# Layer 0's remaining modulation begins beside RWKV's first chunks instead of at once

## The chip, the cores and the metric

The kernel runs on one core of one Trainium2 chip. The metric is the device time of one execution in microseconds (us), less is better. One launch computes two layers.

## What is computed

The reference is a trunk of two layers over 512 latent tokens and 256 context tokens (T = 768) of 1024 channels. Each layer, in short:

```python
s_lat = jax.nn.silu(c)
s_ctx = jax.nn.silu(c_ctx)
...
for l in range(DEPTH):
    m_lat = jnp.split((s_lat @ w_mod[l] + b_mod[l])[:, None, :], 6, axis=-1)
    m_ctx = jnp.split((s_ctx @ w_mod[l] + b_mod[l])[None, None, :], 6, axis=-1)
    h_lat = _modulate(x_lat, m_lat[0], m_lat[1])       # x * (1 + scale) + shift
    ...
    y_ctx, y_lat = _mixing_sublayer(...)               # four mixers of one projection, gated and merged
    x_lat = _layer_norm(ALPHA * x_lat + m_lat[2] * y_lat, ln1_g[l], ln1_b[l])
    f_lat = _sq_relu_mlp(_modulate(x_lat, m_lat[3], m_lat[4]), w_ff1[l], w_ff2[l])
    x_lat = _layer_norm(ALPHA * x_lat + m_lat[5] * f_lat, ln2_g[l], ln2_b[l])
    ...
```

The mixers are mLSTM, RWKV-7, latent attention (MLA) and RG-LRU. The modulation depends on `c` and `c_ctx` alone. Shift 1 and scale 1 of a layer (blocks 0 to 3 of 512 columns each) are needed before its input projection; the other blocks, 4 to 11, only after its mixers.

## The kernel before

Tokens lie along the free axis, channels over the 128 partitions. A weight tile of 1024 x 128 (512 KB) is loaded on SP's queue into one of the buffers `wraw` (L343), split by ACT (`whi`, L302) and DVE (`wlo`, L303) into two parts, and multiplied in three passes into PSUM (`mm3`, all by L389). The modulation's loads use the same `wraw` buffers and the same queue.

**The modulation.** `modulation` (L430) lists 48 units for each layer: 12 blocks of 512 columns in 4 quarters of the input. Layer 0's blocks 0 to 3 come first, in `first_mod`, ahead of the mixers. `more_mod` (L442) takes units off the list; `mod_unit` (L447) does one: a load of 512 KB on SP (L450), then four operations on DVE that add weight x c into two accumulators `modacc`, one for the latent tokens' c and one for the context's (L458 starts a block, L460 goes on). With a block's last quarter, small matmuls of `modacc` with a column of ones sum over the partitions into `pq` (by L389), and DVE adds the bias (L498). Layer 0 has 32 units left when its mixers begin, 128 accumulations on DVE.

**The mixers.** `mixers` (L600) writes the program of four threads, one piece at a time: RWKV (`rwkv`, L1429), the modulation (`mod_thread`), the foreground (LRU, latent attention MLA, mLSTM, the gates, one after the other) and a filler. Each thread yields a latency. `now` is an estimate of PE's time, the sum of the work written so far; a thread is taken up again when `now` has passed the time at which it yielded plus its latency, and of the ready ones the first in the list goes. With `mpos=0` the modulation is the first. Its own first yield is `mstart`; then it writes one unit for each `mod=6.6` of `now`.

What is written in this way is then ordered for each engine by the scheduler of the framework, ahead of the run; on the chip each engine executes its own list in order and waits by semaphores. So a unit of the modulation can stand ahead of, or between, the DVE work of a mixer.

**The mixers' steps that the text speaks of.** In the LRU (L963 to L1005) ACT and DVE pass a tile back and forth (L980 and L985 on DVE, L982 to L991 on ACT, with DVE's L990 to L997 behind). RWKV's projections are evicted from PSUM by L1417 to L1419 on ACT and shifted on DVE (L1422, L1425); L1489 on DVE reads PSUM that the first product of the chunks needs (`kpz`). RWKV then goes through six groups of chunks; L1574 begins a group on DVE. Beside them runs MLA's softmax: DVE takes the row's largest (L1095) and scales it (L1096), ACT makes the exponential and its sum (L1098), DVE the reciprocal (L1100), POOL divides (`p`, L1101), and PE transposes the result (`pq`, L400). After the chunks RWKV's output is normed (`ky`, L1501 to L1512). The mLSTM works on two pairs of heads; at the end of each, DVE forms the output `hs` (L1353 to L1364) and its norm with ACT (L1384 to L1392, ACT's square L1388), and PE transposes it. ACT's decay exponentials `mde` (L1250) are the mLSTM's as well.

Of the kernel before, what the change touches and what calls it, by code (L numbers as in the profile page):

```python
# [137 lines left out]
def _layout(inp):  # L138
# [73 lines left out]
    for d in range(2):  # L212
        for gi, nm in enumerate(("lru_wa", "lru_wx")):
            for t in range(2):
# [22 lines left out]
PARM = (  # L237
         dict(rw0=0.3, rw1=0.1, lru=1.7, mla0=2, mla1=0.7, mlp=0.462, ml0=0.66, ml1=0.785, ga=4, sp=3, g3=10,
              g1=0.462, mod=6.6, left=219, left0=136, hr=0, hm=0, hf=0, hw=50, fm0=5, fm1=6, cs=1, dl=1, nr=1, lns=2,
              hl0=0, hl1=0, hl2=0, hres=0, hx=0, pw1=146, pw2=2, mpos=0, mstart=0),  # L240
         dict(rw0=0.099, rw1=0.3, lru=2.8, mla0=1.96, mla1=1.705, mlp=2.38, ml0=2.785, ml1=2.36, ga=2, sp=1.18,
              g3=10, g1=0.809, mod=16.8, left=146, left0=0, hr=0, hm=0, hf=0, hw=50, fm0=5, fm1=6, cs=0, dl=1, nr=0,
              lns=2, hl0=0, hl1=0, hl2=0, hres=0, hx=0, pw1=0, pw2=0, mpos=3, mstart=60),
# [1555 lines left out]
```

## Time and profile before

| | |
|---|---|
| median of 3 runs | 2747.7 us (2746.25 to 2752.73) |
| profiled execution | 2745.26 us, its span 2743.5 us |
| granted TensorE clock, mean | 0.974 of full speed |
| busy: PE, DVE, ACT, POOL | 2587.3, 1546.2, 1029.6, 441.8 us |
| DMA | 300.07 MB, 109 GB/s mean |

Busy shares are of the span. PE is TensorE, ACT the Scalar engine, DVE the Vector engine, POOL GpSimd, SP the queue that issues the DMAs. Layer 0's mixers begin at about 48 us of the span; RWKV's chunk groups begin at 182, 266.5, 333, 391.5, 454.5 and 507 us and end at 611.5; the first mLSTM pair ends near 656 us.

### The profile page before, as it was taken

How to read it: one execution, taken by the hardware profiler on the slowest of the kernel's cores; microseconds unless marked ns; L12 is line 12 of the kernel's file. 1: busy time of each engine (PE TensorE's matmuls, PEld its weight loads, DVE VectorE, ACT ScalarE, POOL GpSimd, SP SyncE). 2: the span in 40 equal slices, each digit the busy share in tenths (PEclk: the TensorE clock that was granted, in tenths of full speed). 3: DMA queues.
4: the chain of work that ended last, by engine and by line, in shares of the span. 5: the costliest groups of instructions: out<-in, count | busy, mean ns of one | idle time of the engine just before them, and what ended most of it. 6: DMA issues, size and time to landing. Idle time of an engine off the chain costs nothing. (4 is left out here: it accounts for less than half of the span.)

```text
span 2743.5 us, 53586 instructions
## 1 busy us (share of the span) xinstructions
PE 2587.3 (94%) x22980; PEld 2112.7 (77%) x22980; DVE 1546.2 (56%) x2627; ACT 1029.6 (38%) x1642; POOL 441.8 (16%) x420
## 2 busy tenths in 40 slices
PE   7999999998999999999999988999999899999997
PEld 4777776777888878888888867666776778888887
DVE  6885775554354377555553575565665355833335
ACT  3653334335222244121213366543433433622324
POOL 0110212211023132010202200111211113211111
PEclk9999998999999999999999999899999999999998
DMA  7452331133263323434342242211122356333333
GB/s 267 149 176 65 98 96 31 51 90 111 83 215 97 122 85 123 125 121 123 119 125 72 89 136 92 90 52 55 50 73 84 115 177 205 116 100 99 94 99 101
DMA packets 117581, 300.07 MB, mean 109 GB/s; under 512 B 11056, under 2 KB 38064, under 8 KB 117344
## 3 DMA queue, kind: packets, MB, share of 16 engines
q1 hardware_dynamic: 117344, 296.66, 34.1%
q8 instruction: 180, 2.95, 0.4%
q14 instruction: 57, 0.47, 0.1%
HBM read 261.60 MB, written 34.91 MB: 108 GB/s over the span
## 5 line engine op out<-in xcount | busy, mean ns | idle before, releaser
L302 ACT ACTIVATE whi<-wraw 128x1024 fp32r<-128x1024 f32 x295 | 312.0, 1058 | 957.0 <-PE m L389 718.4
L389 PE MATMUL m<-hhi,whi 128*128 128x256 f32 (+1 forms) x2000 | 601.6, 362 | 21.7 <-ACT mk L1273 5.9
L389 PE MATMUL m<-hlo,whi 128*128 128x256 f32 (+1 forms) x2000 | 591.0, 356 | 2.7 <-DVE hlo L921 2.1
L389 PE MATMUL m<-hhi,wlo 128*128 128x256 f32 (+1 forms) x2000 | 588.4, 355 | 0.7 <-DVE wlo L303 0.7
L303 DVE TENSOR_TENSOR wlo<-wraw,whi 128x1024 fp32r<-128x1024 f32 x291 | 367.8, 1265 | 382.3 <-ACT whi L302 371.6
L389 PEld LDWEIGHTS m<-hhi,whi 128*128 128x128 f32 x2000 | 379.0, 191 | 86.3 <-issue 8.2
L389 PEld LDWEIGHTS m<-hlo,whi 128*128 128x128 f32 x2000 | 381.1, 191 | 59.2 <-DVE hlo L921 4.7
L389 PEld LDWEIGHTS m<-hhi,wlo 128*128 128x128 f32 x2000 | 380.1, 191 | 55.6 <-issue 3.2
L460 DVE SCALAR_TENSOR_TENSOR modacc<-wraw,ccs,modacc 128x512 f32<-128x512 f32 x296 | 223.9, 805 | 41.1 <-DMA wraw<-wmod 41.1
L818 POOL TENSOR_TENSOR rl<-rl 128x512 f32<-128x512 f32 (+2 forms) x73 | 117.8, 1614 | 706.1 <-ACT rl L817 661.9
L389 PE MATMUL m<-fhi,whi 128*128 128x256 f32 (+1 forms) x608 | 175.8, 340 | 1.1 <-ACT fhi L302 1.1
L389 PE MATMUL m<-flo,whi 128*128 128x256 f32 (+1 forms) x608 | 175.5, 340 | 0.2 <-DVE flo L303 0.2
L389 PE MATMUL m<-fhi,wlo 128*128 128x256 f32 (+1 forms) x608 | 175.0, 339 | 0.0
L719 POOL TENSOR_TENSOR gth<-gth 128x768 f32<-128x768 f32 (+1 forms) x48 | 82.9, 1749 | 346.2 <-DVE gth L715 344.3
L794 DVE SCALAR_TENSOR_TENSOR x<-m,dvec,x 128x512 f32<-128x512 f32 (+1 forms) x92 | 53.9, 607 | 128.6 <-PE m L389 128.3
L389 PEld LDWEIGHTS m<-fhi,whi 128*128 128x128 f32 x608 | 113.7, 188 | 15.1 <-ACT fhi L302 1.3
L389 PEld LDWEIGHTS m<-flo,whi 128*128 128x128 f32 x608 | 114.3, 188 | 13.8 <-DVE flo L303 0.6
L389 PEld LDWEIGHTS m<-fhi,wlo 128*128 128x128 f32 x608 | 114.5, 188 | 13.4
L303 DVE TENSOR_TENSOR flo<-rl,fhi 128x512 fp32r<-128x512 f32 (+2 forms) x73 | 55.2, 757 | 82.7 <-ACT fhi L302 82.6
L302 ACT ACTIVATE fhi<-rl 128x512 fp32r<-128x512 f32 (+2 forms) x73 | 49.1, 673 | 112.8 <-POOL rl L818 112.8
L389 PE MATMUL m<-osp,whi 128*128 128x256 f32 (+1 forms) x328 | 79.6, 353 | 6.8 <-DVE osp L303 3.2
L1101 POOL TENSOR_SCALAR p<-p,fst 128x768 f32<-128x768 f32 (+1 forms) x40 | 40.4, 1010 | 250.3 <-DVE fst L1100 210.6
(436 smaller groups left out, 4407.9 us busy)
## 6 DMA issues: line engine op xcount, KB each, us to landing
wraw<-wf SPq DMA_DIRECT2D x145, 512.0 KB, 3.6
wraw<-win SPq DMA_DIRECT2D x106, 512.0 KB, 4.2
wraw<-wmod SPq DMA_DIRECT2D x85, 512.0 KB, 3.6
wraw<-wout SPq DMA_DIRECT2D x28, 512.0 KB, 3.7
kwin<-rkv SPq DMA_DIRECT2D x20, 512.0 KB
gd<-gth SPq DMA_DIRECT2D x23, 384.0 KB, 3.6
gth<-gd SPq DMA_DIRECT2D x23, 384.0 KB, 4.5
wraw<-wbr SPq DMA_DIRECT2D x16, 512.0 KB
```

The source lines that it names most:

```text
L302: self.nc.scalar.activation(hi, src, AF.Copy)
L303: (self.nc.gpsimd if pool else self.nc.vector).tensor_tensor(lo, src, hi.bitcast(F32), op=ALU.subtract)
L389: self.nc.tensor.matmul(out, lhsT=lhsT, rhs=rhs, start=start, stop=stop)
L460: nc.vector.scalar_tensor_tensor(acc, w, c, acc, op0=ALU.mult, op1=ALU.add)
L719: nc.gpsimd.tensor_tensor(self.z[dt][:, q0:T], self.z[dt][:, q0:T], th[:, q0:T], op=ALU.add)
L794: nc.vector.scalar_tensor_tensor(x[et][:, a:b], ps[:, a + off:b + off], gm[:, et, j:j + 1], x[et][:, a:b], op0=ALU.mult, op1=ALU.add)
L818: nc.gpsimd.tensor_tensor(rl[:, a:b], rl[:, a:b], rl[:, a:b], op=ALU.mult)
L1101: nc.gpsimd.tensor_scalar(p[:, 0:nk], p[:, 0:nk], st[:, 3:4], 0.0, op0=ALU.mult, op1=ALU.add)
```

## The change

One number: in layer 0's parameters (`PARM[0]`, L240) `mstart` goes from 0 to 110. The modulation's thread then waits until the other threads have written 110 us of PE work by the program's own estimate, and only then begins with its 32 units, one for each 6.6 us as before. What each unit does stays as it is.

```diff
--- before.py
+++ after.py
@@ -237,7 +237,7 @@
 PARM = (
          dict(rw0=0.3, rw1=0.1, lru=1.7, mla0=2, mla1=0.7, mlp=0.462, ml0=0.66, ml1=0.785, ga=4, sp=3, g3=10,
               g1=0.462, mod=6.6, left=219, left0=136, hr=0, hm=0, hf=0, hw=50, fm0=5, fm1=6, cs=1, dl=1, nr=1, lns=2,
-              hl0=0, hl1=0, hl2=0, hres=0, hx=0, pw1=146, pw2=2, mpos=0, mstart=0),
+              hl0=0, hl1=0, hl2=0, hres=0, hx=0, pw1=146, pw2=2, mpos=0, mstart=110),
          dict(rw0=0.099, rw1=0.3, lru=2.8, mla0=1.96, mla1=1.705, mlp=2.38, ml0=2.785, ml1=2.36, ga=2, sp=1.18,
               g3=10, g1=0.809, mod=16.8, left=146, left0=0, hr=0, hm=0, hf=0, hw=50, fm0=5, fm1=6, cs=0, dl=1, nr=0,
               lns=2, hl0=0, hl1=0, hl2=0, hres=0, hx=0, pw1=0, pw2=0, mpos=3, mstart=60),
```

The diff shows one number; the program that follows from it differs in the order of the instructions on each engine, from the start of the mixers to the second mLSTM pair. Three places on DVE show it. A row is line, operation, output, inputs and shape.

The first is early in the mixers, in the LRU's first half beside RWKV's projections; `ls`, `ltq` and `ll` are the LRU's tiles, `modacc` the modulation's, and - is before, + the change.

```order
 L1425 TENSOR_TENSOR cqgd<-cqgd,ktmp 128x512
-L460 SCALAR_TENSOR_TENSOR modacc<-wraw,ccs,modacc 128x512 x3
+L980 TENSOR_SCALAR ls<-lth,dvec 128x768
 L1452 TENSOR_SCALAR cqgd<-cqgd 64x768
-L980 TENSOR_SCALAR ls<-lth,dvec 128x768
-L460 SCALAR_TENSOR_TENSOR modacc<-wraw,ccs,modacc 128x512
-L303 TENSOR_TENSOR wlo<-wraw,whi 128x1024
 L985 TENSOR_SCALAR ltq<-ltq 128x768
-L460 SCALAR_TENSOR_TENSOR modacc<-wraw,ccs,modacc 128x512 x5
-L990 TENSOR_TENSOR ll_625<-ll_625,ltq 128x768
-L460 SCALAR_TENSOR_TENSOR modacc<-wraw,ccs,modacc 128x512
+L990 TENSOR_TENSOR ll_581<-ll_581,ltq 128x768
```

Ten accumulations (x3, one, x5, one) leave this stretch, five of them from right ahead of L990, and L980 moves up by one place.

The second is in RWKV's fourth chunk group, where MLA's softmax runs beside it; `fst` holds the softmax's row values, `kt` is RWKV's. Before:

```order
L1095 TENSOR_REDUCE fst<-m_4732 128x1
L1100 RECIPROCAL fst<-fst 128x1
L1689 TENSOR_TENSOR kt<-kp_4663,cst 128x256
L1096 TENSOR_SCALAR fst<-fst 128x1
L1095 TENSOR_REDUCE fst<-m_4882 128x1
L1096 TENSOR_SCALAR fst<-fst 128x1
L1694 TENSOR_TENSOR kt<-kt,kp_4697 128x256
L1100 RECIPROCAL fst<-fst 128x1
L1695 STREAM_TRANSPOSE kt<-kt 128x256
L1095 TENSOR_REDUCE fst<-m_4949 128x1
```

With the change, at the corresponding place:

```order
L1695 STREAM_TRANSPOSE kt<-kt 128x256
L460 SCALAR_TENSOR_TENSOR modacc<-wraw,ccs,modacc 128x512
L1095 TENSOR_REDUCE fst<-m_4911 128x1
L1689 TENSOR_TENSOR kt<-kp_4629,cst 128x256
L1096 TENSOR_SCALAR fst<-fst 128x1
L460 SCALAR_TENSOR_TENSOR modacc<-wraw,ccs,modacc 128x512 x2
L1694 TENSOR_TENSOR kt<-kt,kp_4663 128x256
L1100 RECIPROCAL fst<-fst 128x1
L460 SCALAR_TENSOR_TENSOR modacc<-wraw,ccs,modacc 128x512
L1695 STREAM_TRANSPOSE kt<-kt 128x256
L460 SCALAR_TENSOR_TENSOR modacc<-wraw,ccs,modacc 128x512
```

Accumulations now stand between L1096 and L1100 of a softmax row and ahead of the next row's L1095, where there were none.

The third is the end of the first mLSTM pair; `ky` and `kn` are RWKV's output and its norm, `hs`, `mht` and `mhn` the mLSTM's. Before:

```order
L1363 TENSOR_TENSOR mht<-pn,mdn 128x384
L1510 TENSOR_TENSOR ky<-ky,kn_7052 128x256
L1364 TENSOR_TENSOR hs<-hs,mht 128x384
L1512 TENSOR_TENSOR ky<-kpw,ky 128x256
L1509 SCALAR_TENSOR_TENSOR ky<-ky,vec_80,kn_7051 128x512
L1384 TENSOR_REDUCE mhn<-hs 128x12
L1510 TENSOR_TENSOR ky<-ky,kn_7052 128x512
L1385 TENSOR_SCALAR mhn<-mhn 128x12
L303 TENSOR_TENSOR wlo<-wraw,whi 128x1024
L1512 TENSOR_TENSOR ky<-kpw,ky 128x512
L1386 TENSOR_TENSOR hs<-hs,mhn 128x768
```

With the change:

```order
L1363 TENSOR_TENSOR mht<-pn,mdn 128x384
L1364 TENSOR_TENSOR hs<-hs,mht 128x384
L1384 TENSOR_REDUCE mhn<-hs 128x12
L1385 TENSOR_SCALAR mhn<-mhn 128x12
L1386 TENSOR_TENSOR hs<-hs,mhn 128x768
L1389 TENSOR_REDUCE mhn<-msq 128x12
L303 TENSOR_TENSOR wlo<-wraw,whi 128x1024
L1392 TENSOR_TENSOR hs<-hs,mhn 128x768
```

RWKV's rows of `ky` and a weight's `wlo` are no longer between L1363 and L1386; they stand ahead of them.

## Rows read from the trace of the kernel before

**Rows 1.** The page, busy time by engine and share of the span.

```profile
PE 2587.3 (94%) x22980; PEld 2112.7 (77%) x22980; DVE 1546.2 (56%) x2627; ACT 1029.6 (38%) x1642; POOL 441.8 (16%) x420
```

**Rows 2.** Windows, by stage: stretch, length, busy by engine (instructions), clock, DMA share, GB/s.

```profile
48.00:182.00 134.00, 123.56 (x696) 100.65 (x696) 116.06 (x163) 79.27 (x95) 14.24 (x29) 0.94 0.45 144
...
266.50:333.00 66.50, 59.57 (x1110) 46.38 (x1110) 53.64 (x116) 21.95 (x52) 12.50 (x12) 0.97 0.36 109
333.00:391.50 58.50, 53.85 (x1078) 42.36 (x1078) 41.31 (x98) 19.20 (x44) 10.54 (x11) 0.97 0.31 97
391.50:454.50 63.00, 59.44 (x1014) 42.90 (x1012) 38.58 (x86) 24.76 (x59) 10.89 (x14) 0.93 0.17 54
454.50:507.00 52.50, 48.72 (x1005) 37.56 (x1004) 28.63 (x79) 21.20 (x55) 11.79 (x14) 0.93 0.09 23
```

**Rows 3.** The same windows, tile modacc alone: PE, PEld, DVE, clock, DMA share, GB/s.

```profile
48.00:182.00 134.00, 3.46 (x96) 3.12 (x96) 44.97 (x64) 0.94 0.45 144
182.00:266.50 84.50, 2.16 (x64) 2.03 (x64) 10.43 (x17) 0.94 0.34 111
266.50:333.00 66.50, 1.14 (x34) 1.01 (x32) 22.43 (x32) 0.97 0.36 109
333.00:391.50 58.50, 2.15 (x64) 2.03 (x64) 10.59 (x16) 0.97 0.31 97
```

**Rows 4.** PE's waits, 48 to 182 us: releaser, us in total, times, longest.

```profile
PE m L389 <- ACT kwdad L1419: 3.9, 1, 3.9
PE m L389 <- ACT kk L1419: 2.5, 1, 2.5
```

**Rows 5.** Timeline, 82.5 to 91.2 us: start, length, instruction, idle before.

```profile
82.59 3.40 DVE L460 SCALAR_TENSOR_TENSOR modacc<-wraw,ccs,modacc 128x512 f32<-128x512 f32 x5
...
84.22 0.94 ACT L989 ACTIVATE ltq<-ltq,cbias 128x768 f32<-128x768 f32 x1
...
85.90 0.96 DVE L990 TENSOR_TENSOR ll<-ll,ltq 128x768 f32<-128x768 f32 x1
...
90.85 0.80 PE L389 MATMUL m<-xc,lruw 128*128 128x256 f32 x1 [3.94 <-ACT kwdad L1419]
```

**Rows 6.** Windows of 20 us, columns as in the windows by stage.

```profile
80.00:100.00 20.00, 16.06 (x69) 12.48 (x68) 17.80 (x23) 15.66 (x19) 2.04 (x1) 0.83 0.50 154
...
180.00:200.00 20.00, 17.90 (x108) 15.15 (x108) 14.81 (x31) 6.27 (x15) 3.31 (x3) 0.74 0.67 229
...
640.00:660.00 20.00, 13.20 (x66) 11.24 (x65) 14.11 (x17) 15.09 (x34) 8.62 (x6) 0.84 0.45 141
```

**Rows 7.** PE's waits, 182 to 391.5 us.

```profile
PE pq L400 <- POOL p L1101: 7.3, 7, 2.9
PE kpz L389 <- DVE kr L1489: 2.3, 1, 2.3
```

**Rows 8.** PE's waits, 391.5 to 520 us.

```profile
PE pq L400 <- POOL p L1101: 0.3, 1, 0.3
```

**Rows 9.** Line L1101, 182 to 392 us: durations in ns, min/median/max.

```profile
L1101 POOL TENSOR_SCALAR p<-p,fst x10: 905/1346/2135, 257.4 to 371.2; 128x768 f32<-128x768 f32 x8, 128x256 f32<-128x256 f32 x2
```

**Rows 10.** Line L1101, 392 to 520 us.

```profile
L1101 POOL TENSOR_SCALAR p<-p,fst x13: 478/905/1742, 394.3 to 519.9; 128x768 f32<-128x768 f32 x8, 128x256 f32<-128x256 f32 x5
```

**Rows 11.** Timeline of DVE, end of the first mLSTM pair.

```profile
639.05 0.55 DVE L1363 TENSOR_TENSOR mht<-pn,mdn 128x384 f32<-128x384 f32 x1
...
641.18 2.22 DVE L1364 TENSOR_TENSOR hs<-hs,mht 128x384 f32<-128x384 f32 x1
...
647.58 0.94 DVE L1386 TENSOR_TENSOR hs<-hs,mhn 128x768 f32<-128x768 f32 x1
```

**Rows 12.** Timeline of ACT, the same place.

```profile
641.00 2.99 ACT L1250 ACTIVATE mde<-mde,mtk 128x128 f32<-128x128 f32 x9 [0.16 <-POOL mde L1246]
648.56 0.84 ACT L1388 ACTIVATE msq<-hs 128x768 f32<-128x768 f32 x1 [4.56 <-DVE hs L1386]
```

**Rows 13.** Timeline of PE, the same place.

```profile
655.21 1.09 PE L400 MATMUL pq<-cst,hs 128*128 128x128 f32 x4 [6.80 <-DVE hs L1392]
```

## The prediction

> **What bounds the kernel now.** I read the page's busy times first: PE is busy 94% of the span, DVE 56%, ACT 38% [rows 1]. So a microsecond is won or lost only where PE stands still or runs at its lower clock; a busy microsecond saved on DVE is worth nothing by itself. The reader should look for two things: where DVE is so full that PE waits for it, and where it is not.
>
> The windows by stage show that [rows 2]. From 48 to 182 us, where the LRU's and RWKV's projections run, DVE is busy 116.06 of 134 us, and PE 123.56. Later DVE has room: 38.58 of 63 us in RWKV's fourth chunk group (391.5 to 454.5) and 28.63 of 52.5 in its fifth (454.5 to 507). The same windows for the tile modacc alone [rows 3] say what fills the first stretch: 64 accumulations, 44.97 us, 0.70 us each. The next three stages hold 17, 32 and 16 of them, 65 in all, and after 391.5 us layer 0 has none.
>
> PE's waits in the first stretch are few [rows 4]: 3.9 us for kwdad and 2.5 us for kk, both by ACT's line L1419; one more, 2.3 us for kr by DVE, stands at its end, at 182 us [rows 7]. They cost more than themselves: in the 20-us windows with the first and the last of them the granted clock is 0.83 and 0.74 [rows 6], as part of PE's work behind each wait ran at 1.2 GHz and not at 2.4. The missing shares, 0.17 and 0.26 of 20 us, are 8.6 us.
>
> **What the change moves.** No instruction is added or removed. By the order of DVE's program, 48 accumulations (the work of 12 of the 32 loads; 48 x 0.70 = 33.7 us of DVE) leave the first stretch. The first three chunk groups hold 68 of them where they held 64, and the fourth and fifth, which had none, now hold 28 and 16, 44 together. The 12 loads of 512 KB go with them on SP's queue. The matmuls that follow the accumulations move too, 96 in 3.46 us in the first stretch [rows 3], 36 ns each; PE does them either way: nothing. From the second mLSTM pair on the two programs read alike, so the span after about 660 us stays as it is.
>
> **1. The first stretch, waits: -2.3 us.** The wait of 3.94 us at 90.85 [rows 5] ends a chain in which ACT does the LRU's steps and then L1419. DVE's five accumulations (3.40 us from 82.59) stand ahead of L990, for which ACT's next step waits; in the order of the change they are gone from there. But L990 also needs ACT's L989, which ends at 84.22 + 0.94 = 85.16, so it can start 0.7 us sooner than 85.90, not 3.4. I take 0.7 of 3.9 (bounds 0 and 3.9). For the wait of kk a third, 0.8 of 2.5 (bounds 0 and 2.5): accumulations ahead of L980 go there in the same way, ACT's chain stays. For kr at 182 us the order of the change still has four accumulations right ahead of L1489, where three stood; only what DVE has caught up before counts, again a third, 0.8 of 2.3 (bounds 0 and 2.3). Sum 2.3 of 8.7, about a quarter.
>
> **2. The same stretch, clock: -2.2 us.** A quarter of the waits, a quarter of the 8.6 us [rows 6]. Bounds: 0, if each shortened wait still lowers the clock, and 8.6, if none does. I stay near the first, since three quarters of the waiting are left.
>
> **3. Chunk groups four and five, waits: +5.1 us.** The nearest row is the softmax's division p on POOL, line L1101, which PE's transposes wait for: 7.3 us in 7 waits between 182 and 391.5 us, where 65 accumulations stand beside it [rows 7], and 0.3 us in 391.5 to 520, where there are none [rows 8]. Ahead of each division DVE has L1095, L1096 and L1100, and the change puts accumulations between these (the order, second place). So (7.3 - 0.3) x 44/65 = 4.7, and 7.3 x 4/65 = 0.4 for the four that the first groups gain. Below: 0, since DVE is busy only 61% and 55% of the two groups and gets 44 x 0.70 = 31 us more in 115.5 us [rows 2], which leaves it at 85%. Above: each of the 13 divisions there waits as long as those seven did on the mean, 1.04 us, 13.6 - 0.3 = 13.3 us. I take the proportional value because it comes from the same instructions beside the same neighbour, a hundred microseconds earlier. On SP's queue the loads stand ahead of chunk inputs; the DMA share there is 0.17 and 0.09 [rows 2], which covers them: 0, at most the four accumulations of one load (2.8 us) for which a buffer is held, once in each group, 5.6.
>
> **4. The same groups, clock: +2.0 us.** From 266.5 to 391.5 us the clock is 0.97 [rows 2], 3.75 us missing of 125, beside 9.6 us of waits of this kind (7.3 and 2.3, [rows 7]): 0.4 us for one of waiting, 5.1 x 0.4. Bounds 0 and, at 13.3 us, 5.3.
>
> **5. The end of the first mLSTM pair: -3.4 us.** PE waits 6.80 us at 655.21 for hs [rows 13]. DVE's half of the chain for it runs from L1363 at 639.05 to the end of L1386 at 648.52 [rows 11], 9.5 us; the steps of RWKV's output stand between its members, and L1364 takes 2.22 us, four times L1363 of the same shape. In the order of the change those steps are all ahead of L1363 (third place). That they are gone, and L1364 takes what L1363 does, shortens this half by at most 9.5 less 3.1 (two of 0.55, two of about 0.94 and a small one): 6.4. But ACT's square L1388 now stands behind 22 of the mLSTM's decay exponentials where nine did. Nine took 2.99 us, so 13 more take 4.3, of the 4.56 us that ACT stood idle before the square [rows 12]: if ACT comes no sooner to them, 0.3 is left. I take the middle of 0.3 and 6.4, 3.4; bounds 0 and 6.8. **Its clock** is 0.84 in 640 to 660 [rows 6], 3.2 us missing; half of the wait goes, so half of that: -1.6 (bounds 0 and 3.2).
>
> **Sum.** -2.3 - 2.2 + 5.1 + 2.0 - 3.4 - 1.6 = -2.4 us. Against the profiled execution (2745.26, its span 2743.5 and 1.8 around it) that is 2742.9; that execution lies 2.4 below the median of the runs shown, 2747.7, so the forecast for the median is **2745.3**. A measurement of this kernel can tell about 0.3%, 8.2 us, from no change, so this counts as none.
>
> **A rule weighed.** The division L1101 has a median of 1346 ns where accumulations run beside it and 905 ns where there are none [rows 9, 10], 0.44 us apart. The Trainium skill, page "SBUF — State Buffer", section "Who interferes with whom", has a reason for it: a DVE instruction with two SBUF inputs, as the accumulation is, contends with a GpSimd instruction that reads SBUF, and whoever starts first holds the shared port pair for the whole instruction. The two medians agree with it. By that rule alone, an estimate of step 3's 4.7 is 13 x 0.44 = 5.7 us, and 2746.3 in all. It speaks against the change.
>
> **Rivals.** *The three stalls of the first stretch shrink below what slows PE.* DVE loses 33.7 of 116 us there, and a queue that empties may give back more than the one chain that I followed. Then all but half a microsecond of each wait goes, 8.7 - 1.5 = 7.2, and the 8.6 of clock, with steps 3 to 5 as they are: -7.2 - 8.6 + 7.1 - 5.0 = -13.7, **2734.0**. For it: DVE's share of that stretch, and that ACT waits on DVE step by step. Against: L990 gains 0.7 only, and four accumulations still stand ahead of L1489. Chance 0.26.
>
> *POOL and the softmax become the bound in groups four and five.* Each division there waits as those of 182 to 391.5 us did, behind accumulations on DVE's queue and lengthened beside them on POOL: +13.3, clock +5.3; the tail gains nothing, as ACT's exponentials hold it; the first stretch gives its -4.5. Together +14.1, **2761.8**. It decides from about 9 us of waits for p after 391.5 us on. For it: 1346 against 905 ns, and the places where an accumulation stands between L1096 and L1100. Against: DVE is half idle there. Chance 0.17.
>
> *The change does nothing that PE sees.* The waits of the first stretch are ACT's and stay, the softmax has slack, as the 0.3 us show, and the tail waits for the exponentials: **2747.7**. Chance 0.12.
>
> **How the numbers follow.** The forecast has 0.45; its own range, from most of the first stretch's gains with the losses as priced to the losses at twice their price, is 2736 to 2753: 0.11 of the 0.45 lies more than 8.2 us below 2747.7, 0.31 within, 0.03 above. The first rival is faster (0.26), the second slower (0.17), the third the same (0.11) or just slower (0.01). Faster 0.37, same 0.42, slower 0.21. The range takes in most of the first rival and reaches towards the second, 2731 to 2758, and leaves about 0.1 out on either side.
>
> **What would show it.** Step 1: the waits for kwdad, kk and kr at about 3.2, 1.7 and 1.5 us; step 2: the clock of 80 to 100 and of 180 to 200 us a little above 0.83 and 0.74 (the first rival: above 0.95 both). Steps 3 and 4: waits for p of 5 us after 391.5 us, L1101's median there near 1.3 us, the two groups longer by 7 us together. Step 5: a wait of about 3.4 us for hs by L1392. The forecast is wrong if the first stretch gives over 12 us, if the waits for p pass 9 us, or if the span after the second mLSTM pair differs by more than 3 us.

## The result and the profile after

The change makes the kernel slower: 2774.97 us (median of 5 runs, 2761.24 to 2778.65) against 2747.7 (5 runs, 2746.01 to 2752.73), ratio 1.0081, 95% interval 1.0054 to 1.0109. On two other chips the same kernel came out at 1.0044 (1.0026 to 1.0062) and 1.0028 (1.0009 to 1.0047), so the loss is 0.3 to 0.8% by where it is measured, and a loss each time: 27.3, 11.4 and 8.1 us over the median of the kernel before there. 2745.3 was forecast, 2731 to 2758, which is 2.4 us less than the kernel before, 16.7 less to 10.3 more.

The profiled execution took 2778.65 us, its span 2776.9. The page's busy times, as in [rows 1]:

```profile
PE 2616.3 (94%) x22980; PEld 2134.3 (77%) x22980; DVE 1545.0 (56%) x2627; ACT 1029.7 (37%) x1642; POOL 444.2 (16%) x420
```

PE executes the same 22980 matmuls in 29.0 us more of busy time than before (2587.3), while DVE, ACT and POOL are busy for as long as they were. So 29.0 of the 33.4 us by which the span grew are busy time of PE and not waits. The span and the mean granted clock of the core, before and after, say where it is:

```profile
core 0: 2743.5 us, clock 0.974
```

```profile
core 0: 2776.9 us, clock 0.962
```

Span times clock is 2672.2 us before and 2671.4 after. Counted at full clock the two executions are equally long, and the whole difference is that PE ran at 1.2 GHz for more of it. This is not one execution alone: over the five runs of the change the product is 2672.0 on the mean, over 27 runs of the kernel before on another chip 2672.3.

The windows by stage show where the clock went (stretches between the same marks as in [rows 2]: RWKV's groups begin at 175, 256.3, 319.9, 391, 462.6 and 521.7 us; the last row is the end of the first mLSTM pair):

```profile
48.00:175.00 127.00, 115.75 (x605) 94.62 (x601) 87.34 (x119) 79.21 (x96) 10.79 (x29) 0.97 0.33 106
175.00:256.30 81.30, 78.62 (x1024) 61.97 (x1024) 46.39 (x85) 32.45 (x53) 8.58 (x10) 0.98 0.35 109
256.30:319.90 63.60, 57.75 (x1105) 44.54 (x1104) 49.52 (x108) 19.93 (x48) 10.29 (x11) 0.99 0.34 105
319.90:391.00 71.10, 64.70 (x1068) 49.30 (x1067) 41.83 (x101) 21.31 (x50) 13.13 (x13) 0.76 0.23 70
391.00:462.60 71.60, 65.63 (x1061) 48.10 (x1059) 57.16 (x124) 24.27 (x56) 16.05 (x15) 0.88 0.28 88
462.60:521.70 59.10, 52.36 (x1062) 42.39 (x1061) 41.04 (x96) 21.73 (x53) 11.53 (x12) 0.86 0.29 83
632.30:686.80 54.50, 48.20 (x258) 37.94 (x257) 35.04 (x60) 35.65 (x75) 16.71 (x9) 0.87 0.45 143
```

The first stretch is shorter, 127 us for 134, at 0.97 for 0.94, and the first two groups keep their clock. Then the third group has 0.76 where it had 0.97: 0.24 x 71.1 = 17.1 us of full clock missing where 1.8 were. The fourth and fifth miss 8.6 and 8.3 us, where they missed 4.4 and 3.7. PE also stands still for longer there: 6.0 and 6.7 us in these two groups for 3.6 and 3.8, and 6.4 in the third for 4.7 (each group's length less PE's busy time).

In the third group nothing waits at the place where most is lost. This window is within it:

```profile
318.00:338.50 20.50, 20.50 (x130) 13.63 (x131) 9.66 (x30) 7.43 (x20) 1.52 (x1) 0.50 0.06 21
```

PE is busy for all of the 20.5 us, at half rate throughout, DVE for less than half of them, and the same window for modacc has no accumulation at all. At half rate the same work takes twice as long, and the ends of matmuls are modelled in this profile, so that nothing waits there is in part a consequence of the low clock. The clock fell at 318.2 us, when PE had been busy for 25 of the 28 us before and had three matmuls of a projection still to do. What differs from the kernel before is PE's work. The windows for the tile m alone (foreground work, mostly the wide matmuls of projections), third group, before and then after (columns PE, PEld, DVE, ACT, POOL, clock):

```profile
333.00:391.50 58.50, 27.20 (x110) 17.42 (x110) 3.12 (x5) 4.74 (x10) 0.00 (x0) 0.97 0.31 97
```

```profile
319.90:391.00 71.10, 23.06 (x67) 12.43 (x66) 4.03 (x6) 6.28 (x14) 0.00 (x0) 0.76 0.23 70
```

110 such matmuls became 67; the order of the programs has 103 and 57. One input projection of 48 matmuls, a gate's, has left the group, and wide work between RWKV's narrow products has become rare: from the end of the projection at 320 us on PE has none until 366.5. This lies in how the threads are dealt out. In the loop of `mixers`, with `now` in us, the filler, which is last in the list, has its turns, from the sixth on, at

```
before: 241.7  265.9  296.0  315.8  408.3
after:  231.4  282.2  302.9  398.5
```

The modulation's thread is first in the list and now takes its turns until later; the filler has come to eight gates when `now` is 316, where it had come to nine, and to the ninth only at 398.5. No instruction was added, but PE's order changed by one projection, which the diff doesn't show and which the prediction never counted.

Up to the second pair's first transpose, PE has executed 7831 matmuls in both kernels; from there on the programs are the same:

```profile
0.00:675.00 675.00, 618.31 (x7831) 477.30 (x7832) 443.70 (x905) 285.95 (x517) 100.30 (x136) 0.95 0.35 114
675.00:2743.50 2068.50, 1969.03 (x15151) 1635.42 (x15149) 1102.46 (x1722) 743.65 (x1126) 341.46 (x284) 0.98 0.34 108
```

```profile
0.00:700.60 700.60, 638.85 (x7831) 491.11 (x7832) 443.52 (x905) 286.01 (x517) 103.81 (x136) 0.92 0.34 110
700.60:2776.90 2076.30, 1977.42 (x15151) 1643.23 (x15149) 1101.44 (x1722) 743.70 (x1126) 340.36 (x284) 0.98 0.34 107
```

25.6 us of the 33.4 between these two executions are ahead of the mark (20.5 of them PE's busy time for the same matmuls), 7.8 behind it, in instructions that the change doesn't touch: the clock of one execution scatters by that much. So does the third group: in two more executions of the same program (e0, e15, below) it had 0.87 and 0.85 and not 0.76, with the falls at other places, so the row of 318 to 338.5 us is the worst of three.

### The profile page after: what moved, and what is told of

The parts are those of the page before. It is cut to its first block, busy times and chain, and to the rows that moved or that the text cites. A ratio compares the mean times of both kernels' runs of the same rounds, so it can differ in the third digit from the quotient of the medians.

```text
span 2776.9 us, 53597 instructions
## 1 busy us (share of the span) xinstructions
PE 2616.3 (94%) x22980; PEld 2134.3 (77%) x22980; DVE 1545.0 (56%) x2627; ACT 1029.7 (37%) x1642; POOL 444.2 (16%) x420
## 5 line engine op out<-in xcount | busy, mean ns | idle before, releaser
L1101 POOL TENSOR_SCALAR p<-p,fst 128x768 f32<-128x768 f32 (+1 forms) x40 | 44.3, 1107 | 259.0 <-DVE fst L1100 226.8
```

The lines of the kernel that those rows point to most:

```text
L1101: nc.gpsimd.tensor_scalar(p[:, 0:nk], p[:, 0:nk], st[:, 3:4], 0.0, op0=ALU.mult, op1=ALU.add)
```

## The experiments

Two theories to begin with. *Accumulation theory*: the accumulations beside RWKV's later groups delay DVE, PE stalls, and the clock falls behind the stalls; this is what steps 3 and 4 were made of. *Order theory*: the clock falls because PE's foreground work is dealt out otherwise; after eight runs it was narrowed to the *hole theory*: the clock falls in a third group without its gate projection, some 45 us in which PE has no wide projection. In each, the number of accumulations by stage and of m by group is counted in the order of the kernel's program.

**Shrink the accumulations (e1).** In the changed kernel:

```diff
-                    nc.vector.scalar_tensor_tensor(acc, w, c, acc, op0=ALU.mult, op1=ALU.add)
+                    (lambda y: nc.vector.scalar_tensor_tensor(y(acc), y(w), c, y(acc), op0=ALU.mult, op1=ALU.add))((lambda t: t[:, 0:64] if l == 0 and blk > 3 else t))
```

> The changed kernel, with the accumulations L460 of layer 0's blocks 4 to 11 cut from 512 columns to 64 (their sums are then incomplete). The order on PE keeps the changed kernel's share of foreground matmuls m by chunk group (57 in the third, where the kernel before has 103). Order theory (the loss comes from how PE's foreground work is dealt out among the chunk groups, which lets PE's clock fall): stays slow, 2765 to 2780 us, third group's clock under 0.85. Accumulation theory (the loss comes from DVE's accumulations beside the chunk groups, which delay the softmax and RWKV's steps): back to the time before or under it, 2735 to 2750 us.

2764.76 us, ratio 1.0057 (1.003 to 1.0085), mean clock of its runs 0.9668 against 0.9721. In the third group the accumulations take 5.29 us for 11.29:

```profile
325.40:385.70 60.30, 2.88 (x64) 2.80 (x64) 5.29 (x17) 0.91 0.25 79
```

The loss stays although the work beside the groups is gone by half and more. That speaks against the accumulation theory, though the clock here (0.91) is above the change's, and above the 0.85 that the order theory had set as the most.

**Shift the estimate, not the modulation (e2, e3).** The modulation's matmuls add to `now`; a small number added there deals the threads out otherwise. e2, in the changed kernel, and e3, in the kernel before:

```diff
-            pq = self.fp("pq")
+            pq = self.fp("pq"); self.pe -= 1.1
```

```diff
-            pq = self.fp("pq")
+            pq = self.fp("pq"); self.pe += 1.2
```

> The changed kernel, with 1.1 taken off the estimate of PE's time for each finished block of the modulation. Accumulations stay placed as in the changed kernel (36, 16, 32, 22, 26, 16 by stage), but the foreground's m on PE are dealt out as before: 106, 103, 71, 37 in groups two to five against 104, 57, 71, 40 in the changed kernel. Order theory: fast again, 2735 to 2750 us, third group's clock about 0.97. Accumulation theory: stays at 2765 to 2780 us.

> The kernel before (accumulations begin at once, none after the third group), with 1.2 added to the estimate of PE's time for each finished block. The foreground's m are dealt out otherwise: 108, 58, 116, 17 in groups two to five. Order theory: slower than before, 2755 to 2775 us, with the third group's clock under 0.9. Accumulation theory: as before, 2742 to 2752 us.

e2: 2757.77 us, ratio 1.0028 (1.0008 to 1.0048), mean clock 0.9725, that of the kernel before (0.9721) with the accumulations as late as in the change; so late accumulations alone did not lower it. But e2 isn't free: the 7.0 us that it is over before on the mean are all in span times clock (2680.1 against 2672.3), so in waits. e3: 2755.15, ratio 1.0017 (0.9994 to 1.004), clock 0.9717. Its third group has 58 m and no fall: against the order theory in its first form.

**Begin at 109, at 140 and at 40 (e4, e6, e7).** `mstart=109`, `140`, `40` in place of 110.

> The changed kernel with mstart 109 in place of 110. Accumulations by stage 36, 22, 26, 32, 16, 16, nearly the same; m on PE 106, 112, 57, 37, 312, 168 in groups two to six and behind, where the changed kernel has 104, 57, 71, 40, 352, 117. Order theory: the third group keeps its clock (over 0.95); in all 2738 to 2755 us. Accumulation theory: as the changed kernel, 2765 to 2780 us.

> The changed kernel with mstart 140: the modulation begins still later (accumulations 28, 19, 21, 32, 27, 21 by stage), but the m on PE are 137, 104, 114, 21 in groups two to five, 239 in groups three to five. Order theory: mean clock 0.971 or over, time 2740 to 2755 us. Accumulation theory: clock as with the change or lower, 0.965 or under, 2765 to 2785 us.

> The changed kernel with mstart 40: accumulations 64, 20, 32, 20, 12, 0 by stage, so close to the kernel before, with m on PE as in the changed kernel: 104, 57, 70, 33 in groups two to five, 160 in groups three to five. Order theory: mean clock 0.963 to 0.968, 10 to 25 us slower than before. Accumulation theory: near the time before, at most a quarter of the change's loss (12 of 44 accumulations), 2748 to 2756 us.

e4: 2753.15, ratio 1.0011 (0.9992 to 1.003): one unit of `mstart` less, with 112 m in the third group, and no loss is left that is clear of the interval. e6: 2754.93, ratio 1.0016 (1.0003 to 1.0028); the clock is lower than before (0.9687 against 0.9713), as the accumulation theory has it, but span times clock is 4.7 us lower as well. e7: 2763.83, ratio 1.0055 (1.0035 to 1.0074), clock 0.9663: nearly all accumulations are early, the third group has 57 m (clock 0.81), and the loss is there.

**The change again (e0), and few m with early accumulations (e5).** e5 is the kernel before with `self.pe -= 0.6` at the same place as e3.

> The changed kernel itself, on the same chip as the runs below. Both theories: slower than before by 15 to 30 us, mean clock about 0.964 where the kernel before has 0.972, span times mean clock as before (2672 us).

> The kernel before, with 0.6 taken off the estimate of PE's time for each finished block. Accumulations stay exactly where they were by stage (84, 22, 26, 16, 0, 0); the foreground's m on PE become 106, 104, 22, 36 in groups two to five, 162 in groups three to five where the kernel before has 199 and the changed kernel 168. Order theory (fewer m between the chunk steps of groups three to five let the clock fall): mean clock 0.963 to 0.968, 10 to 25 us slower than before. Accumulation theory: clock and time as before, within 5 us.

e0: 2762.48, ratio 1.0044 (1.0026 to 1.0062), clock 0.9686 against 0.9713, span times clock 2674.0 against 2670.7: a smaller loss than the 15 us at least that were expected, and 3.3 us of it are not clock. e5: 2750.22, ratio 1.0004 (0.9986 to 1.0021). With 162 m in groups three to five it should have lost by the order theory; it keeps its projection in the third group (104). Hence the hole theory.

**Move gate projections (e8, e9, e10).** In the filler; e8 in the changed kernel (factor 0.2 after the seventh gate), e9 and e10 in the kernel before (factor 3 after the sixth, the eighth); e9's edit is shown:

```diff
-            yield self.parm["g3"] * (self.parm["g1"] if n == 1 else 1)
+            yield self.parm["g3"] * (self.parm["g1"] if n == 1 else 1) * (3 if self.l == 0 and len(self.parked) == 6 else 1)
```

> The changed kernel, with the filler's seventh wait cut to a fifth, so that it writes its eighth gate projection earlier. Accumulations 36, 16, 32, 24, 24, 16 by stage, as with the change; m on PE 104, 65, 109, 32 in groups two to five, where the changed kernel has 104, 57, 71, 40: about one projection (48 m) comes to groups three and four. Order theory, as it stands after the first eight runs (the clock falls in a third group that has lost its gate projection, unless the fourth gets it): mean clock back to 0.970 or over, within 6 us of the kernel before. Accumulation theory: stays where the change is, clock 0.967, 10 to 25 us over the kernel before.

> The kernel before, with the filler's sixth wait three times as long. Accumulations where they were (84, 22, 26, 16, 0, 0); m on PE 106, 48, 30, 36 in groups two to five, where the kernel before has 106, 103, 69, 27: the third group loses a gate projection and the fourth does not get it. Order theory: mean clock 0.964 to 0.968, 10 to 25 us over the kernel before. Accumulation theory: clock 0.972 and time as before, within 5 us.

> The kernel before, with the filler's eighth wait three times as long. Accumulations where they were; m on PE 106, 103, 21, 27 in groups two to five: the third group keeps its projection, the fourth loses one. Order theory: as e5, whose fourth group had 22: clock 0.970 or over, within 5 us of before; if the fourth group counts as the third does, 10 us or more slower. Accumulation theory: as before, within 5 us.

e9: 2776.45, ratio 1.0066 (1.0043 to 1.0088). Nothing of the modulation has moved here, and it is as slow as the change. Its third group:

```profile
331.00:396.60 65.60, 56.98 (x1040) 43.36 (x1039) 42.37 (x103) 19.87 (x47) 13.51 (x15) 0.79 0.29 86
```

But of its 20.8 us on the mean only some 8 are clock (0.9682 against 0.9711); span times clock is 12 over before. And it moves more than one projection: the fourth group loses one as well, and up to the second mLSTM pair's first transpose PE has 7639 matmuls, 192 (four projections) fewer than before. e10: 2753.02, ratio 0.9996 (0.9978 to 1.0014): a projection less in the fourth group costs nothing. e8: 2765.72, ratio 1.0034 (1.0013 to 1.0055), clock 0.9681: the projection came to the fourth group, the third stayed without one, and the loss stayed; the order theory, as it then stood, had expected it gone.

**Put the projection back (e11, e12).** In the changed kernel (e12 with 255):

```diff
-            t = ready[0]
+            t = ready[-1] if self.l == 0 and len(self.topark) == 18 and now > 260 else ready[0]
```

> The changed kernel, with one gate projection of the filler put into the third chunk group by force (where the estimate has passed 260 and 18 gates are left to park). Accumulations 36, 16, 32, 22, 26, 16 as with the change; m on PE 105, 104, 71, 40, 352, 117, the changed kernel's row but for 48 m more in the third group, where it has 57. Hole theory (the change takes one gate projection out of the third group and leaves some 45 us of PE without wide matmuls, in which the clock falls): mean clock 0.970 or over, at most 6 us over the kernel before. Accumulation theory: clock 0.967, 10 to 25 us over it.

> As e11, with the projection forced where the estimate has passed 255; m on PE 104, 106, 70, 40, 352, 117. Hole theory: as e11, clock 0.970 or over, at most 6 us over the kernel before. Accumulation theory: clock 0.967, 10 to 25 us over it.

e11: 2759.25, ratio 1.0013 (0.9994 to 1.0032), clock 0.9709 against 0.9715. e12: 2760.96, ratio 1.0018 (1.0 to 1.0035), clock 0.9697. By median they are 6.7 and 8.4 us over before, where 6 at most were expected. **Side by side on one chip (e15, e16)**, the change and e11's kernel:

> The changed kernel, on the same chip as e16, so that the two can be set side by side. Hole theory: ratio to the kernel before 1.004 to 1.008, mean clock under 0.969, and over e16 by 0.002 or more in the ratio. Accumulation theory: the same ratio as e16 within 0.001.

> The kernel of e11 (the change with one gate projection put back into the third group), on the same chip as e15. Hole theory: ratio 0.9995 to 1.003, mean clock 0.970 or over. Accumulation theory: as e15.

e15: 2764.1, ratio 1.0028 (1.0009 to 1.0047), clock 0.9669 against 0.9703 of the kernel before, span times clock equal (2672.3 and 2672.0). e16: 2761.33, ratio 1.002 (1.0002 to 1.0039), clock 0.9703: the mean clock is back in full. The time is not. The ratios differ by 0.0008, where the hole theory expected 0.002 or more and the accumulation theory at most 0.001; on the mean e15 is 10.0 us over before and e16 still 5.7, as its span times clock is 5.3 us over. One wait is larger than that, the same in e11. PE's waits in e16's third group, and the row of POOL and of DVE at it:

```profile
PE pq L400 <- POOL p L1101: 10.4, 4, 8.0
```

```profile
345.53 7.53 POOL L1101 TENSOR_SCALAR p<-p,fst 128x768 f32<-128x768 f32 x1 [1.59 <-DVE fst L1100]
```

```profile
345.67 6.70 DVE L460 SCALAR_TENSOR_TENSOR modacc<-wraw,ccs,modacc 128x512 f32<-128x512 f32 x10
```

A division whose median is 905 ns with no accumulation beside it [rows 10] takes 7.53 us beside ten accumulations in a row, and PE stands for 7.99 us. By the Trainium skill, page "SBUF — State Buffer", section "Who interferes with whom", a DVE instruction with two SBUF inputs and a GpSimd instruction that reads SBUF exclude each other; this trace agrees, and shows a division held for a whole row of ten. Who came first it doesn't show: the division's start is recorded 0.14 us ahead of the first accumulation's.

The third group in the profiled executions, of the change (e0, e15), with the projection put back (e16, e12), and of e3:

```profile
320.50:386.90 66.40, 57.75 (x1068) 44.83 (x1067) 41.94 (x103) 21.31 (x50) 13.71 (x13) 0.87 0.24 73
316.90:383.30 66.40, 58.99 (x1068) 46.22 (x1067) 41.89 (x103) 21.34 (x50) 13.73 (x13) 0.85 0.24 72
318.20:394.60 76.40, 62.92 (x1117) 49.93 (x1114) 43.00 (x105) 21.66 (x52) 18.01 (x13) 0.89 0.22 69
317.70:387.10 69.40, 61.80 (x1118) 48.14 (x1117) 44.02 (x105) 21.61 (x50) 11.92 (x13) 0.95 0.26 80
318.50:381.20 62.70, 52.18 (x1089) 39.94 (x1088) 44.42 (x104) 24.22 (x53) 12.30 (x13) 0.97 0.28 84
```

In e16 the group misses 8.4 us of full clock, hardly less than in e0 and e15 (8.6 and 10.0), and e11 has the same 0.89: the wait of 8 us stands in the middle of the projection that was put back, with the low clock from 348.7 us on. So where e16 won its mean clock the traces don't show. e12, whose projection comes earlier, keeps 0.95.

**Fill the stretch of groups four and five (e13, e14).** The same line, with two gates forced (after `now` = 340 and 370) in the kernel before, and with these and e11's in the changed one.

> The kernel before, with two gate projections forced into its own stretch without projections in groups four and five (85 us in its trace, 17 us of it at 1.2 GHz). m on PE 106, 103, 119, 67, 325, 96 in place of 106, 103, 69, 27, 319, 96. Hole theory: mean clock 0.974 or over and 4 to 9 us faster than before. If only the third group counts: as before, within 3 us.

> The changed kernel with three gate projections forced, one into the third group as in e11, two into groups four and five as in e13; accumulations as with the change. Hole theory: mean clock 0.973 or over, 3 to 10 us faster than the kernel before. Accumulation theory: clock 0.968 or under, slower than before by 8 us or more.

e13: 2758.6, ratio 1.0019 (0.9998 to 1.004), clock 0.9681: lower, not higher. e14: 2759.4, ratio 1.0023 (1.0002 to 1.0044), clock 0.9713. The hole theory had expected both to be faster than before; on the mean they are 7.2 and 8.3 us slower. More m in the chunk groups is not a remedy as such: in e13 the clock fell behind the filled place instead, in the fifth group, where from 488.6 to 502.3 us PE has no projection and two m, at half rate:

```profile
461.50:529.00 67.50, 62.38 (x1048) 48.10 (x1047) 31.96 (x82) 22.97 (x57) 12.03 (x14) 0.85 0.11 32
```

**The accumulations at their old place (e17).** e1's edit in the kernel before.

> The kernel before, with the accumulations L460 of layer 0's blocks 4 to 11 cut from 512 columns to 64 (their sums are then incomplete); m on PE as in the kernel before. Hole theory: the accumulations cost little where the dealing of m is kept, 0 to 8 us faster than the kernel before, clock as before. Accumulation theory: 10 us or more faster, clock over 0.974.

2751.02, ratio 0.9992 (0.9969 to 1.0015), clock 0.9705 against 0.9703: where no projection moves, an eighth of the columns is worth at most a few microseconds.

All together, for kernels by whether the third group holds a gate projection:

| third group | kernels | ratio to the kernel before |
|---|---|---|
| none (48 to 65 m) | the change (three chips), e1, e7, e8, e9 | 1.0081, 1.0044, 1.0028, 1.0057, 1.0055, 1.0034, 1.0066 |
| none | e3 | 1.0017 |
| kept or put back (103 to 112 m) | e2, e4, e5, e6, e10, e11 and e16, e12, e13, e14, e17 | 1.0028, 1.0011, 1.0004, 1.0016, 0.9996, 1.0013 and 1.002, 1.0018, 1.0019, 1.0023, 0.9992 |

What is shown: the change's loss is granted clock, nearly all of it (10 of 10 us on one chip, 8 of 11 on another). The mean clock of the runs follows the way in which PE's work is dealt out and not the place of the accumulations: with these late but the dealing as before the mean clock is that of before (e2), with the dealing of the change it is low though they are early (e7) or an eighth as wide (e1). Putting one projection back gives the mean clock back (e16 for e15, 0.0033 more).

What is not shown is that the empty third group itself is the cause. It fits most rows of the table and the place of the falls in the change, but e3 keeps its clock with an empty third group, e6 and e13 lose some of it with a full one, and in e11 and e16 the third group is no better in the traces. Without the projection PE also stands still for longer in that group (6.4, 8.7 and 7.4 us in the three executions of the change, 8.8 in e7 and 8.6 in e9, for 4.7 before), so a clock that falls behind waits isn't excluded as the way in which the hole acts; e3, which stands still for 10.5 us there at 0.97, speaks against it, but no run was made to separate the two.

Late accumulations have a price of their own. With them late and the projection in its place, e2, e11, e12, e14 and e16 are still 5.7 to 8.3 us slower than before on the mean, most of it in span times clock (2.9 to 7.8 us over) and so in waits, of which the 8 us is the one that was found (e4 and e6 lose only 2.3 and 2.8). And in the profiled executions groups four and five miss some 17 us of full clock on the mean of eleven that have full accumulations in both (10 to 24), some 9 on that of eight that have none or narrow ones (5 to 15). No version beat the kernel before by more than its interval; e16's order with the division off POOL was not tried.

## Why the prediction was wrong, step by step

The view that failed stands ahead of the steps, in "What the change moves": it counted DVE's rows by stage and SP's loads and took PE's work as merely moved ("PE does them either way: nothing"). The order of PE was open to be counted in the same way, and would have shown 57 m for 103 in the third group. That this would have given the sign of the loss is not sure: e3 has 58 and keeps its clock.

**Step 1** (-2.3 us of waits). The three waits named shrank as expected and more:

```profile
PE kpz L389 <- DVE kr L1489: 2.1, 1, 2.1
PE m L389 <- ACT kwdad L1419: 1.3, 1, 1.3
PE m L389 <- ACT cqgd L1419: 1.2, 1, 1.2
PE m L389 <- ACT kr L1419: 1.2, 1, 1.2
PE m L389 <- ACT kk L1419: 1.2, 1, 1.2
```

8.7 became 4.6, and kr kept 2.1, with the four accumulations that the order shows right ahead of it. But a wait of 1.2 for cqgd is new, that for kr by ACT grew from 0.2 to 1.2, and another of 0.7 is new: PE's time not busy is 11.3 us (127 less 115.75), where it was 10.4 (134 less 123.56). The waits were spread, not shortened, so in sum the step failed. **Step 2** (-2.2 of clock) was right in sign and too small: the missing clock of the stretch fell from 8.0 to 3.8 us.

```profile
80.00:100.00 20.00, 18.66 (x101) 15.41 (x100) 10.01 (x11) 17.11 (x20) 1.25 (x1) 1.00 0.10 27
180.00:200.00 20.00, 17.99 (x145) 15.00 (x144) 19.23 (x39) 9.35 (x12) 3.29 (x3) 0.91 0.70 235
```

Of the 7 us that the stretch is shorter, 3.4 are the modulation's matmuls that left it, which come again later.

**Step 3** (+5.1 of waits for p). Right in the place, wrong in the balance: 3.3 us after 391, where 0.3 were, and in the first three groups 3.1, where 7.3 were. First these earlier groups, then the later two, with the division's durations in ns (min/median/max):

```profile
PE pq L400 <- POOL p L1101: 3.1, 5, 1.0
L1101 POOL TENSOR_SCALAR p<-p,fst x11: 829/933/1965, 248.1 to 370.6; 128x768 f32<-128x768 f32 x8, 128x256 f32<-128x256 f32 x3
```

```profile
PE pq L400 <- POOL p L1101: 3.3, 4, 1.1
L1101 POOL TENSOR_SCALAR p<-p,fst x11: 479/1251/1988, 403.7 to 511.0; 128x768 f32<-128x768 f32 x8, 128x256 f32<-128x256 f32 x3
```

In sum 6.4 for 7.6. That all of PE's waits in groups four and five grew by 5.4 us (12.7 for 7.3) is near the 5.1 by luck, as only 3.0 of it is the wait that was priced. The medians of the division went the way of the rule that was weighed, 1251 ns after 391 us, though 933 before, where the groups hold 65 accumulations as they did: whether a division meets one depends on the order, not on the count alone. With accumulations of 64 columns the earlier median, 1346 in the kernel before, is 911:

```profile
L1101 POOL TENSOR_SCALAR p<-p,fst x10: 482/911/1593, 256.9 to 370.9; 128x768 f32<-128x768 f32 x8, 128x256 f32<-128x256 f32 x2
```

The two medians that the prediction compared mix the shapes otherwise (2 small divisions of 10, 5 of 13), which it did not allow for.

**Step 4** (+2.0 of clock) is the step that failed. It priced the clock by the waits, 0.4 us for one of waiting, and in groups four and five alone; and that price came from 9.6 us of waits beside the clock of 266.5 to 391.5 us, though 2.3 of them, for kr, stand at 182 us, outside that stretch. The profiled execution showed 8.8 us more missing in the fourth and fifth groups, beside 5.4 us more of waits, and 15.3 more in the third, which the step left out, as no accumulation was added there, and where PE's waits grew by 1.8. So the clock didn't follow the length of the waits at that price; with the waits alone, and PE's order as before (e2), the mean clock did not fall. Which property of PE's order makes it fall stays open, as said above.

**Step 5** (-3.4 and -1.6). The wait for hs went from 6.80 to 1.37:

```profile
686.83 0.41 PE L400 MATMUL pq<-cst,hs 128*128 128x128 f32 x2 [1.37 <-DVE hs L1392]
```

and 2.9 us for ky, which now comes earlier, took half of it back. The clock there fell to 0.87 from 0.94 (58.5 us before), where a gain was forecast. **The rest** of the program was to stay within 3 us and differs by 7.8, by the scatter of the clock. **The rivals**: the second one named the right sign (2761.8, chance 0.17) by the wrong mechanism, since waits for p stayed at 3.3 us, far from the 9 that were to decide. Of the first, the clock of 80 to 100 us came true (1.00 for 0.83), that of 180 to 200 nearly (0.91 for 0.74, over 0.95 expected), and was outweighed; its three waits were to go to half a microsecond each, and two of them stand at 1.2 to 1.3 and one at 2.1.

## What to carry over

Where a program is dealt out by an estimate of time, a change to one thread moves the others: count every engine's work by stage in the new order, TensorE's first, before pricing the part that was meant to move. Multiply the span by the mean granted clock before looking for waits; if the products agree, the added time is not the length of waits, though a wait may still stand ahead of a fall of the clock. And a difference of this size should be tried at neighbouring values of the same number (109 beside 110) before it is put down to what the number is named for.

## What was not expected of the hardware

PE can be at 1.2 GHz for 20.5 us in which the profile has it busy for all of the time (the window of 318 to 338.5 us); it had been at full clock up to 318 us, and the work there is RWKV's narrow products with 16 matmuls m (10.36 of the 20.5 us). The Trainium skill, page "TensorE: Matmul & The Clock Gate", section "Part 1: The HAM clock gate", describes a gate that sustained matmul activity opens; being busy in the profile's sense was not enough here. One program's clock scatters more than the change costs: the kernel before ran from 2738.55 to 2767.16 us in 27 runs on one chip, mean clock 0.966 to 0.978. And a POOL division, 905 ns by its median with no accumulation beside it [rows 10], took 7.53 us beside ten accumulations of DVE.
